# A post-norm layer (mLSTM and pooling mixer, squared-ReLU MLP): a pool of its own for the first norm's scale and bias, six weight loads held back, the second MLP product in another order

## The chip, the core and the metric

The kernel runs on one core of one Trainium2 chip. The metric is the device time of one execution in microseconds (us). The engines are TensorE (PE: matmuls, and transposes through the matmul array), VectorE (DVE), ScalarE (ACT), GpSimd (POOL) and SyncE (SP, which here only issues loads). Each runs its own list of instructions in order and waits for others by semaphores. DMA queues move data between HBM and the on-chip memory (SBUF); matmuls write to PSUM.

## What is computed

One layer over 1024 tokens of width 1024, all in float32:

```
u = x @ w_in                                  # q, k, v, gates, output gate, pooling columns
h = mLSTM(silu(conv(q)), silu(conv(k)), v, i, f)   # 4 heads x 128, a state carried from chunk to chunk
y_m = sigmoid(output gate) * layer_norm_per_head(h) * hn_g
y_p = (trailing means over 2/4/8/16 - p) @ w_pool * scale
x1 = layer_norm(ALPHA * x + concat(y_m, y_p) @ w_out, ln1_g, ln1_b)
out = layer_norm(ALPHA * x1 + square(relu(x1 @ w_ff1)) @ w_ff2, ln2_g, ln2_b)
```

`w_ff1` is 1024 x 4096, `w_ff2` 4096 x 1024.

## The kernel before, in words

Every matmul operand is split into a high part (a cast on ScalarE, L76) and a low part (a subtraction on VectorE, L77), and each product is three matmuls (L103 to L105, in `mm3`). A column block of 512 takes one such matmul a little over 0.23 us.

**Mixer.** Tokens come in two halves of 512 (`hf`), each of four chunks of 128. The projections run one after another, `proj_o` (output gate), `proj_p` (pooling), `proj_vg` (v and gates), `proj_qk`; beside them lie the tasks put off with `later`, run when `tick` reaches their due step. `mlstm_stages(c)` is a chunk in four steps: decay weights (`ng`, `si`) by GpSimd (L489, L499) and ScalarE (L491); q-k scores on TensorE (L496) and the transposed keys (L503), scaled values `vs` on GpSimd (L507); then the output (L516, L517), copied by ScalarE into `o` (L518), and the state's increment (L524), added on VectorE into `C` (L526 or L530), which the next chunk's L516 reads; on VectorE the norm of `o` to `y` (L535 to L549); last the transposes of `y` (L553). L496, L517 and L524 write PSUM tiles named `ml`, of which there are two. The output gate of a chunk is copied (L234), put through a sigmoid (L238) and multiplied with `hng` by GpSimd (L239). In what follows, "the first chunk's copy" is L518 for chunk 0.

Nearly all working tiles of the mixer (`hng`, `og`, `o`, `y`, `kt`, `vs`, `u`, ...) come from one ring, `bigp`, of 42 tiles: a new tile takes the slot of the oldest and its first writer waits for the last reader of what stood there. A scheduler of the framework puts each engine's instructions in order from these waits and its estimates of their times.

`out_proj` multiplies with `w_out` in two column halves and applies the first norm; for the last two chunks of a half VectorE does it in two steps, L637 (scale, `gs[0:2]`) and L643 (bias, `gs[2:4]`). The four tiles `gs1` (named `lngb`) are scale and bias, spread over partitions by a GpSimd DMA (L915), taken from `bigp`.

**MLP.** After the mixer `bigp` is closed and its room goes to a pool `fq` of 21 tiles. The two matrix products are done in blocks of 512 with seven block products in place of eight; `jobs` lists them as (r, ph, i): four rounds r, phase 0 (`w_ff1`) and 1 (`w_ff2`), and i in the order 1, 2, 5, 6, 3, 7, 4 in the first round. A job has 16 tile steps of three matmuls, 48 in all. `prep(n)` makes the operands of job n and calls `weights` for job n + 1 (n + 2 for n = 0): SyncE loads a base block (L732), GpSimd adds further blocks with accumulating DMAs (L735) where i needs a sum. Two tiles, p = 0 and 1, make a job's weights. `x1_transpose(1, ...)` transposes the last 512 tokens (L660, 32 transposes) at the second job, i = 2; job 3 (i = 5) needs them and a sum of two weight blocks.

Of the kernel before, what the change touches and what calls it, by code (L numbers as in the profile page):

```python
# [22 lines left out]
def trunk_layer(ctx: ExitStack, tc: tile.TileContext, x, w_in, b_gate, w_conv, hn_g,  # L23
# [24 lines left out]
    ps_tr = ctx.enter_context(tc.tile_pool(name="ps_tr", bufs=2, space=bass.MemoryType.PSUM))  # L48
    dram = ctx.enter_context(tc.tile_pool(name="dram", bufs=2, space=bass.MemoryType.DRAM))
    early = ExitStack()  # L50
    bigp = early.enter_context(tc.tile_pool(name="bigp", bufs=42))

    cnt = [0]
    anchor = [None]
# [8 lines left out]
    def sml(shape, tag, bufs=2):  # L63
        return small.tile(shape, F32, tag=tag, name=nm(tag), bufs=bufs)
# [11 lines left out]
        act.copy(hi, src)  # L76
        dve.tensor_tensor(lo, src, hi.bitcast(F32), ALU.subtract)  # L77

    def after(ins, anchor):
        tc.add_manual_dep(  # L80
            ins.ins, anchor.ins.name,
            mybir.DependencyInfo(mybir.DependencyClass.NoSync, mybir.DependencyReason.DATA),
            reason="start of the load")

    def wpiece(src, n, before=None):
# [294 lines left out]
    def gates_stages(hf):  # L380
        g8 = gt[hf]
        iv, fv = g8[:, :, 0:4], g8[:, :, 4:8]
        v3 = lambda t: t.rearrange("p (c h) -> p c h", h=4)
        af, u, lnu, t1 = (sml([P, 16], n) for n in ("g_af", "g_u", "g_ln", "g_t1"))
        lf = sml([P, 16], "g_lf")
        ab = sml([P, 2, 16], "g_ab")
        dve.scalar_tensor_tensor(v3(af), fv, -1.0, fv, op0=ALU.mult, op1=ALU.min)
        act.activation(af, af, AF.Exp)
        dve.tensor_scalar(u, af, 1.0, None, op0=ALU.add)
        act.activation(lnu, u, AF.Ln)  # L390
        dve.scalar_tensor_tensor(t1, u, -1.0, af, op0=ALU.add, op1=ALU.subtract)
        dve.reciprocal(u, u)
        dve.tensor_tensor(t1, t1, u, ALU.mult)
        dve.tensor_tensor(t1, lnu, t1, ALU.subtract)
        dve.scalar_tensor_tensor(v3(lf), fv, 0.0, v3(t1), op0=ALU.min, op1=ALU.subtract)
        yield
        pa = trps([P, 16])
        pe.matmul(pa, lhsT=tri, rhs=lf, start=True, stop=True)
        dve.tensor_copy(ab[:, 0, :], pa)
        dve.tensor_tensor(v3(ab[:, 1, :]), iv, v3(ab[:, 0, :]), ALU.subtract)  # L400
        yield
        pt = trps([16, 2, P])
        for i in range(2):
            pe.transpose(pt[:, i, :], ab[:, i, :], ident)
        abT = big([16, 2, P], name="g_abT")
        dve.tensor_copy(abT, pt)
        cm = big([16, P], name="g_cm")
        dve.tensor_tensor_scan(cm, zcol.to_broadcast([16, P]), abT[:, 1, :], -3.0e38, op0=ALU.add, op1=ALU.max)
        yield
        pr = trps([1, 2, 16])  # L410
        pe.transpose(pr[:, 0, :], abT[:, 0, P - 1:P], ident[:16, :16])
        pe.transpose(pr[:, 1, :], cm[:, P - 1:P], ident[:16, :16])
        row = sml([1, 2, 16], "g_row")
        dve.tensor_copy(row, pr)
        dve.tensor_tensor(row[:, 1, :], row[:, 1, :], row[:, 0, :], ALU.add)
        m = sml([1, 20], "g_m")
        gm = sml([1, 16], "g_gm")
        dve.tensor_copy(m[:, 0:4], mst)
        for c in range(TT):
            s, s2 = slice(4 * c, 4 * c + 4), slice(4 * c + 4, 4 * c + 8)  # L420
            dve.tensor_tensor(gm[:, s], row[:, 0, s], m[:, s], ALU.add)
            dve.tensor_tensor(m[:, s2], gm[:, s], row[:, 1, s], ALU.max)
        dve.tensor_copy(mst, m[:, 16:20])
        rr = sml([1, 2, 16], "g_rr")
        dve.tensor_tensor(rr[:, 0, :], row[:, 0, :], m[:, 4:20], ALU.subtract)
        dve.tensor_tensor(rr[:, 1, :], gm, m[:, 4:20], ALU.subtract)
        yield
        pb = trps([P, 2, 16])
        pe.matmul(pb.rearrange("p a b -> p (a b)"), lhsT=ones, rhs=rr.rearrange("p a b -> p (a b)"),
                  start=True, stop=True)  # L430
        so, ep = sml([P, 16], "g_so"), sml([P, 16], "g_ep")
        act.activation(so, pb[:, 1, :], AF.Exp)
        dve.tensor_tensor(ep, ab[:, 1, :], pb[:, 0, :], ALU.add)
        act.activation(ep, ep, AF.Exp)
        pm = trps([16, 1])
        pe.transpose(pm, m[:, 0:16], ident[:1, :1])
        mp = sml([16, 1], "g_mp")
        dve.tensor_copy(mp, pm)
        gs = big([16, 2, P], name="g_gs")
        dve.tensor_scalar(gs[:, 0, :], cm, mp, -1.0, op0=ALU.max, op1=ALU.mult)  # L440
        act.activation(gs[:, 1, :], gs[:, 0, :], AF.Exp, bias=mp)
        th = big([16, P], name="g_th")
        dve.scalar_tensor_tensor(th, gs[:, 0, :], 0.5 * math.log(P), abT[:, 0, :],
                                 op0=ALU.add, op1=ALU.subtract)
        act.activation(th, th, AF.Exp)
        yield
        pth = trps([P, 16])
        pe.transpose(pth, th, ident[:16, :16])
        thr = sml([P, 16], "g_thr")
        dve.tensor_copy(thr, pth)  # L450
        dr = dram.tile([2, 16, P], F32, tag="bounce", name=nm("bounce"))
        act.dma_start(dr.rearrange("a r t -> r a t"), gs)
        G[hf] = dict(so=so, ep=ep, b=ab, thr=thr, dr=dr)
# [196 lines left out]

    xq = {}

    def x1_transpose(hf, kbs, alloc):
        for kb in kbs:
            if kb % 2 == 0:
                xq[kb // 4, hf, kb % 4 // 2] = alloc()
            t = xq[kb // 4, hf, kb % 4 // 2]
            ps = trps([P, TT, P])
            for j in range(TT):
                pe.transpose(ps[:, j, :], z[hf * TT + j, kb // 4][:, (kb % 4) * P:(kb % 4 + 1) * P], ident)  # L660
            act.copy(t[:, kb % 2, :], ps.rearrange("p j t -> p (j t)"))

    def x_second(j):
# [17 lines left out]
    def quad(name="q"):  # L681
        return fq.tile([P, 2, 512], F32, tag="q", name=nm(name))
# [14 lines left out]

    banks = [lambda: mmps([P, 512]), aux]

    def product(L, R, ps, first, outer="k"):  # L700
        steps = [(p, kk) for p in C2 for kk in C2]
        its = [(s, m) for s in steps for m in range(4)] if outer == "k" else \
            [(s, m) for m in range(4) for s in steps]
        for (p, kk), m in its:
            s = slice(m * P, (m + 1) * P)
            anchor[0] = mm3(ps[m], L[p][0][:, kk, s], L[p][1][:, kk, s], R[p][0][:, kk, :], R[p][1][:, kk, :],
                            first and p == 0 and kk == 0, p == 1 and kk == 1, not first)
# [15 lines left out]

    grown = {}

    def weights(r, ph, i):
        parts = (WQ1, WQ2)[ph][i]
        for p in C2:
            t, have = grown.pop((r, ph, parts[:-1], p), (None, 0)) if len(parts) > 1 else (None, 0)
            if t is None:  # L730
                t = quad("w")
                sp.dma_start(t, w_source(r, ph, parts[0], p))  # L732
                have = 1
            for q in parts[have:]:
                pool.dma_start(t, w_source(r, ph, q, p), accum_op=ALU.add)  # L735
            grown[r, ph, parts, p] = (t, len(parts))
# [74 lines left out]
    def prep(n):  # L811
        r, ph, i = jobs[n]
        if n == 0:
            L, R = firsts[1], firsts["x"]
        elif n == 1:
            L, R = firsts[2], x_right(r, i)
        elif ph == 0:
            L, R = operands(r, ph, i), x_right(r, i)
        else:
            L, R = h_left(i), operands(r, ph, i)  # L820

        k = n + 1 + (n == 0)
        if n != 1 and k < len(jobs):
            weights(*jobs[k])
        return L, R

    def evict1(i, ps):
# [81 lines left out]
    proj_qk(1, 0)  # L909
    later(1, lambda: mlstm(1))  # L910
    proj_p(1)
    gs1 = [big([P, 512], name="lngb") for _ in range(4)]
    for e in range(4):
        src = (ln1_g, ln1_b)[e // 2][0:1, e % 2 * 512:(e % 2 + 1) * 512]
        after(pool.dma_start(gs1[e], src.to_broadcast([P, 512])), anchor[0])  # L915
# [3 lines left out]
    early.close()  # L919
    fq = ctx.enter_context(tc.tile_pool(name="fq", bufs=21, reuse_waits="tile"))  # L920

    ready = prep(0)
    open_ps = {}
    for n, (r, ph, i) in enumerate(jobs):
        L, R = ready
        if n == 1:
            x1_transpose(1, range(KB), lambda: quad("x1"))
        if n + 1 < len(jobs):
            ready = prep(n + 1)
        which = CHAIN[i]  # L930
        if i in FIRST:
            open_ps[which] = [banks[which ^ ph]() for _ in range(4)]
        ps = open_ps[which]
        if (r, ph, i) == (NR - 1, 1, 5):
            for v in (ln2_g, ln2_b):
                t = quad("lngb")
                after(pool.dma_start(t.rearrange("p e c -> p (e c)"), v.to_broadcast([P, 1024])), anchor[0])
                gb2.append(t)
        fin = r == NR - 1 and ph == 1 and i in (2, 3, 7, 4)
        product(L, R, ps, i in FIRST, "m" if fin else "k")  # L940
        if ph == 0:
            evict1(i, ps)
        else:
            evict2(i, ps, r)
# [25 lines left out]
```

## Time and profile before

| | |
|---|---|
| median of 3 runs | 1042.88 us (1039.37 to 1043.12) |
| profiled execution, its own time | 1042.8 us |
| its span in the profile | 1041.1 us |
| mean granted TensorE clock | 0.991 |
| busy: PE, DVE, ACT, POOL | 97%, 71%, 43%, 15% of the span |
| DMA | 141.20 MB, mean 136 GB/s |

A granted clock of 1.00 is 2.4 GHz, 0.50 is 1.2 GHz. A wait is put down to the instruction whose semaphore came last; "<-DVE z L643" means that VectorE's instruction of line 643 on the tile `z` ended it. Where nothing is said, times are us from the start of the span.

### The profile page before, as it was taken

The page shows a single profiled execution, that of the slowest core. Times are in us where ns is not written, and L with a number is a line of the kernel's source. Part 1 is how long each engine was busy: PE and PEld are TensorE (multiplying, and loading weights), DVE is VectorE, ACT ScalarE, POOL GpSimd, SP SyncE. Part 2 cuts the span into 40 slices and gives each one's busy share as a digit, 9 for nine tenths or more (in the row PEclk, how much of TensorE's full clock was granted, in tenths as well). Part 3 has the DMA queues.
Part 4 walks back from the last instruction along what each step waited for, and adds up shares of the span by engine and source line. Part 5 has one row for each costly group of instructions (what it writes and reads, how often), then busy time and mean ns, then how long its engine had stood idle before and what let it go on. Part 6 is the DMA issues. An engine that isn't in the chain of part 4 may idle for free.

```text
span 1041.1 us, 12565 instructions
## 1 busy us (share of the span) xinstructions
PE 1007.4 (97%) x4697; PEld 824.4 (79%) x4697; DVE 734.7 (71%) x1203; ACT 450.7 (43%) x644; POOL 155.4 (15%) x194
## 2 busy tenths in 40 slices
PE   7999999999989998899999999999999999999995
PEld 5898789887868887688888888888888888888884
DVE  5473864977898476768966478966478965478887
ACT  5334555547522134443333534333534333534363
POOL 2320002220330011400302001302001302000211
PEclk9999999999999999899999999999999999999998
DMA  8411503323531147993908953908953908902656
GB/s 294 152 63 41 163 22 92 123 81 101 182 83 58 44 111 233 294 302 92 162 1 180 283 200 64 162 1 185 290 191 62 162 1 187 298 1 42 122 101 203
DMA packets 63518, 141.20 MB, mean 136 GB/s; under 512 B 4620, under 2 KB 4704, under 8 KB 63456
## 3 DMA queue, kind: packets, MB, share of 16 engines
q1 hardware_dynamic: 41328, 91.04, 26.2%
q0 software_dynamic: 21744, 48.79, 23.9%
q8 instruction: 37, 0.61, 0.2%
q10 hardware_dynamic: 384, 0.56, 0.1%
q14 instruction: 25, 0.20, 0.1%
HBM read 126.18 MB, written 11.57 MB: 132 GB/s over the span
## 4 chain that ended last, share of the span: by engine, by line
PE 84%; DVE 8%; DMA 4%; ACT 2%; issue 1%; DVEq 0%; SPq 0%; ACTq 0%; POOLq 0%
PE mm L105 17%; PE mm L103 17%; PE mm L104 17%; PE tr L103 5%; PE tr L104 5%; PE tr L105 5%; PE ml L103 5%; PE ml L104 5%; PE ml L105 5%; DMA w<-in_w_ff_dram 2%; DMA xraw<-in_x_dram 1%; DVE wlo L77 1%; DVE ol L77 1%; DMA xres<-in_x_dram 1%; PE tr L177 1%
## 5 line engine op out<-in xcount | busy, mean ns | idle before, releaser
L77 DVE TENSOR_TENSOR ol<-w,oh 128x1024 fp32r<-128x1024 f32 x112 | 135.7, 1222 | 97.1 <-ACT oh L76 97.0
L76 ACT CAST oh<-w 128x1024 fp32r<-128x1024 f32 x112 | 116.6, 1047 | 153.2 <-PE mm L104 51.1
L103 PE MATMUL mm<-oh,oh 128*128 128x512 f32 x448 | 176.4, 394 | 0.0
L104 PE MATMUL mm<-ol,oh 128*128 128x512 f32 x448 | 176.2, 393 | 0.0
L105 PE MATMUL mm<-oh,ol 128*128 128x512 f32 x448 | 176.2, 394 | 0.0
L735 POOL DMA_DIRECT2D w<-in_w_ff_dram x64 | 77.0, 1287 | 512.8 <-DVE ol L77 476.9
L105 PEld LDWEIGHTS mm<-oh,ol 128*128 128x128 f32 x448 | 84.1, 188 | 19.7
L104 PEld LDWEIGHTS mm<-ol,oh 128*128 128x128 f32 x448 | 84.1, 188 | 19.6
L103 PEld LDWEIGHTS mm<-oh,oh 128*128 128x128 f32 x448 | 84.1, 188 | 19.6 <-DVE h L837 0.2
L103 PE MATMUL ml<-oh,oh 128*128 128x512 f32 x224 | 88.7, 397 | 1.8 <-ACT oh L76 1.8
L103 PE MATMUL tr<-oh,oh 128*128 128x512 f32 x224 | 89.0, 398 | 1.0 <-DVE h L837 0.9
L104 PE MATMUL ml<-ol,oh 128*128 128x512 f32 x224 | 88.6, 396 | 0.9 <-DVE ol L77 0.9
L105 PE MATMUL tr<-oh,ol 128*128 128x512 f32 x224 | 88.9, 397 | 0.0
L104 PE MATMUL tr<-ol,oh 128*128 128x512 f32 x224 | 88.9, 397 | 0.0
L105 PE MATMUL ml<-oh,ol 128*128 128x512 f32 x224 | 88.5, 395 | 0.0
L77 DVE TENSOR_TENSOR ol<-xs,oh 128x1024 fp32r<-128x1024 f32 x42 | 51.4, 1223 | 46.0 <-ACT oh L76 45.7
L76 ACT CAST oh<-h 128x1024 fp32r<-128x1024 f32 x40 | 41.8, 1047 | 79.9 <-PE ml L104 24.6
L76 ACT CAST oh<-xs 128x1024 fp32r<-128x1024 f32 x42 | 44.0, 1048 | 61.6 <-PE ml L104 37.5
L77 DVE TENSOR_TENSOR wlo<-raw,whi 128x1024 fp32r<-128x1024 f32 (+1 forms) x44 | 54.8, 1246 | 17.5 <-ACT whi L76 9.9
L76 ACT CAST whi<-raw 128x1024 fp32r<-128x1024 f32 (+1 forms) x44 | 46.1, 1053 | 34.8 <-PE mm L104 13.8
L103 PE MATMUL mm<-xT,whi 128*128 128x512 f32 x144 | 57.3, 398 | 0.1
L104 PE MATMUL mm<-xT,whi 128*128 128x512 f32 x144 | 57.0, 396 | 0.0
(276 smaller groups left out, 1992.9 us busy)
## 6 DMA issues: line engine op xcount, KB each, us to landing
w<-in_w_ff_dram POOLq DMA_DIRECT2D x64, 512.0 KB, 7.2
w<-in_w_ff_dram SPq DMA_DIRECT2D x58, 512.0 KB, 6.7
xs<-xs SPq DMA_DIRECT2D x42, 512.0 KB, 5.5
raw<-in_w_in_dram SPq DMA_DIRECT2D x28, 512.0 KB, 4.3
xs<-x POOLq DMA_DIRECT2D x12, 512.0 KB, 7.4
raw<-in_w_in_dram SPq DMA_DIRECT2D x8, 520.0 KB, 5.4
raw<-in_w_out_dram SPq DMA_DIRECT2D x8, 512.0 KB, 3.3
xres<-in_x_dram SPq DMA_DIRECT2D x8, 512.0 KB, 3.6
```

The source lines that it names most:

```text
L76: act.copy(hi, src)
L77: dve.tensor_tensor(lo, src, hi.bitcast(F32), ALU.subtract)
L103: pe.matmul(ps, lhsT=lh, rhs=rh, start=start, stop=False, skip_group_check=grow)
L104: pe.matmul(ps, lhsT=lh, rhs=rl, start=False, stop=False, skip_group_check=grow)
L105: return pe.matmul(ps, lhsT=ll, rhs=rh, start=False, stop=stop, skip_group_check=grow)
L177: pe.transpose(ps[:, a, b, :], raw[:, b, kc * P:(kc + 1) * P], ident)
L735: pool.dma_start(t, w_source(r, ph, q, p), accum_op=ALU.add)
```

## The change

Three edits. `gs1` moves from the ring to a pool `gsp` of four tiles; the ring has 39 tiles instead of 42, and ten small tiles of the gate computation have one buffer instead of two. `weights` gets an argument `hold`: with it, SyncE issues a base load only when that matmul has ended; it is the last matmul of job n - 3 in the calls from `prep(n + 1)` for n = 3 to 6. And job 1 (i = 2) is done in parts: the two output tiles m = 1, 3 for three of their four steps (18 matmuls), then the 32 transposes tied behind them, the operands of job 2, the rest of m = 1, 3, then m = 0, 2.

```diff
-    bigp = early.enter_context(tc.tile_pool(name="bigp", bufs=42))
+    bigp = early.enter_context(tc.tile_pool(name="bigp", bufs=39))
+    gsp = early.enter_context(tc.tile_pool(name="gsp", bufs=1))
...
-    def after(ins, anchor):
+    def after(ins, anchor, wait=False):
         tc.add_manual_dep(
             ins.ins, anchor.ins.name,
-            mybir.DependencyInfo(mybir.DependencyClass.NoSync, mybir.DependencyReason.DATA),
+            mybir.DependencyInfo(mybir.DependencyClass.Sync if wait else mybir.DependencyClass.NoSync, mybir.DependencyReason.DATA),
             reason="start of the load")
...
-        af, u, lnu, t1 = (sml([P, 16], n) for n in ("g_af", "g_u", "g_ln", "g_t1"))
-        lf = sml([P, 16], "g_lf")
+        af, u, lnu, t1 = (sml([P, 16], n, 1) for n in ("g_af", "g_u", "g_ln", "g_t1"))
+        lf = sml([P, 16], "g_lf", 1)
...
             for j in range(TT):
-                pe.transpose(ps[:, j, :], z[hf * TT + j, kb // 4][:, (kb % 4) * P:(kb % 4 + 1) * P], ident)
+                t0 = pe.transpose(ps[:, j, :], z[hf * TT + j, kb // 4][:, (kb % 4) * P:(kb % 4 + 1) * P], ident)
+                if start is not None:
+                    after(t0, start)
...
-    def product(L, R, ps, first, outer="k"):
-        steps = [(p, kk) for p in C2 for kk in C2]
-        its = [(s, m) for s in steps for m in range(4)] if outer == "k" else \
-            [(s, m) for m in range(4) for s in steps]
+    STEPS = [(p, kk) for p in C2 for kk in C2]
+
+    def product(L, R, ps, first, outer="k", ms=range(4), steps=STEPS):
+        its = [(s, m) for s in steps for m in ms] if outer == "k" else \
+            [(s, m) for m in ms for s in steps]
...
-                sp.dma_start(t, w_source(r, ph, parts[0], p))
+                load = sp.dma_start(t, w_source(r, ph, parts[0], p))
+                if hold is not None:
+                    after(load, hold, True)
...
-            weights(*jobs[k])
+            weights(*jobs[k], ends[n - 3] if 3 <= n <= 6 else None)
...
-    gs1 = [big([P, 512], name="lngb") for _ in range(4)]
+    gs1 = [gsp.tile([P, 512], F32, name=f"lngb{e}") for e in range(4)]
...
-        if n == 1:
-            x1_transpose(1, range(KB), lambda: quad("x1"))
-        if n + 1 < len(jobs):
+        if n + 1 < len(jobs) and n != 1:
             ready = prep(n + 1)
...
-        product(L, R, ps, i in FIRST, "m" if fin else "k")
+        if n == 1:
+            product(L, R, ps, True, "k", (1, 3), STEPS[:3])
+            x1_transpose(1, range(KB), lambda: quad("x1"), anchor[0])
+            ready = prep(2)
+            product(L, R, ps, True, "k", (1, 3), STEPS[3:])
+            product(L, R, ps, True, "k", (0, 2))
+        else:
+            product(L, R, ps, i in FIRST, "m" if fin else "k")
+        ends.append(anchor[0])
```

**On ScalarE, in the mixer.** The place of the first chunk's copy of its output into the tile `o`. Before, it stands right behind the copies of `v`, and the casts of the weights of `proj_o(1)` (`whi`) follow:

```order
L505 COPY kt_1681<-tr_1676 128x512
L285 COPY v_274_1685<-mm_1687 128x2x128
L285 COPY v_274_1685<-mm_1688 128x2x128
L518 COPY o_1740<-ml_1741 128x258
L518 COPY o_1740<-ml_1745 128x258
L76 CAST whi_1891<-raw_1889 128x1024
L76 CAST whi_1897<-raw_1895 128x1024
L76 CAST whi_2220<-raw_2218 128x1024
L76 CAST whi_2226<-raw_2224 128x1024
```

After (the line numbers are one higher), it stands behind the last copies and sigmoids of the output gate:

```order
L235 COPY og_2209<-mm_2073 128x512
L239 ACTIVATE og_2209<-og_2209 128x512
L235 COPY og_2209<-mm_2074 128x512
L77 CAST whi_2530<-raw_2528 128x1024
L239 ACTIVATE og_2209<-og_2209 128x512
L519 COPY o_1743<-ml_1744 128x258
L519 COPY o_1743<-ml_1748 128x258
L506 COPY kt_1812<-tr_1807 128x512
L286 COPY v_296_1825<-mm_1827 128x2x128
```

The two rows `o<-ml` moved from ahead of eight casts of weights and four copies and four sigmoids of `og` to behind them.

**On TensorE, in the mixer.** The first state increment (`ml<-vs,kt`) and the scores of the next chunk (`ml<-qk,qk`). Before, they stand at the end of a tile pair of `proj_vg(1)`, and that projection's next 48 matmuls (`mm<-whi,xT`) follow:

```order
L517 MATMUL ml_1741<-v_103_593,ng_1599 128x129 x2
L517 MATMUL ml_1745<-v_103_593,ng_1599 128x129 x2
L503 MATMUL tr_1804<-ident,qk_1168 128x128
L524 MATMUL ml_1749<-vs_1683,kt_1681 128x129 x2
L524 MATMUL ml_1753<-vs_1683,kt_1681 128x129 x2
L503 MATMUL tr_1804<-ident,qk_1168 128x128 x3
L496 MATMUL ml_1797<-qk_870,qk_1168 128x128 x4
L103 MATMUL mm_1824<-whi_1521,xT_918 128x256
L104 MATMUL mm_1824<-wlo_1522,xT_918 128x256
L105 MATMUL mm_1824<-whi_1521,xT_918 128x256
```

After, they stand inside the first tile pair of `proj_qk(1, 0)`, and the second chunk's output (`ml<-C,si`) begins right behind the scores:

```order
L104 MATMUL mm_2246<-xT_923,whi_2229 128x512
L525 MATMUL ml_1752<-vs_1686,kt_1684 128x129 x2
L525 MATMUL ml_1756<-vs_1686,kt_1684 128x129 x2
L105 MATMUL mm_2246<-xT_923,whi_2229 128x512
L106 MATMUL mm_2246<-xT_923,wlo_2230 128x512
L104 MATMUL mm_2245<-xT_924,whi_2229 128x512
L497 MATMUL ml_1800<-qk_873,qk_1171 128x128 x4
L517 MATMUL ml_1946<-C_212,si_1610 128x129
L105 MATMUL mm_2245<-xT_924,whi_2229 128x512
L106 MATMUL mm_2245<-xT_924,wlo_2230 128x512
L104 MATMUL mm_2246<-xT_924,whi_2229 128x512
L518 MATMUL ml_1946<-v_112_667,ng_1609 128x129
```

The increment moved past the rest of `proj_vg(1)` and the whole of `proj_o(1)`; between the steps of the first four chunks there now lie mostly three to six matmuls of the projection.

**On TensorE, at the start of the MLP.** The end of the first product (`mm`) and what follows. Before, eight transposes of the last tokens (`tr<-ident,z`):

```order
L104 MATMUL mm_3817<-ol_3728,oh_3404 128x512
L105 MATMUL mm_3817<-oh_3727,ol_3405 128x512
L660 MATMUL tr_3873<-ident,z_3288 128x128
L660 MATMUL tr_3873<-ident,z_3291 128x128
L660 MATMUL tr_3873<-ident,z_3366 128x128
L660 MATMUL tr_3873<-ident,z_3369 128x128
L660 MATMUL tr_3879<-ident,z_3288 128x128
L660 MATMUL tr_3879<-ident,z_3291 128x128
L660 MATMUL tr_3879<-ident,z_3366 128x128
L660 MATMUL tr_3879<-ident,z_3369 128x128
L103 MATMUL ml_3951<-oh_3802,oh_3782 128x512
L104 MATMUL ml_3951<-ol_3803,oh_3782 128x512
```

After, the second product's tiles `ml`:

```order
L105 MATMUL mm_3821<-ol_3731,oh_3407 128x512
L106 MATMUL mm_3821<-oh_3730,ol_3408 128x512
L104 MATMUL ml_3877<-oh_3806,oh_3785 128x512
L105 MATMUL ml_3877<-ol_3807,oh_3785 128x512
L106 MATMUL ml_3877<-oh_3806,ol_3786 128x512
L104 MATMUL ml_3879<-oh_3806,oh_3785 128x512
L105 MATMUL ml_3879<-ol_3807,oh_3785 128x512
L106 MATMUL ml_3879<-oh_3806,ol_3786 128x512
L104 MATMUL ml_3877<-oh_3806,oh_3785 128x512
L105 MATMUL ml_3877<-ol_3807,oh_3785 128x512
```

Eighteen such matmuls now stand ahead of the first transpose; before, they stood behind the first eight.

## Rows read from the trace of the kernel before

**Rows 1.** The page, part 1: busy us of each engine, share of the span, instructions.

```profile
PE 1007.4 (97%) x4697; PEld 824.4 (79%) x4697; DVE 734.7 (71%) x1203; ACT 450.7 (43%) x644; POOL 155.4 (15%) x194
```

**Rows 2.** Stretches: length, busy us (instructions) of each engine, granted clock, DMA share, GB/s.

```profile
177.87:207.00 29.13, 27.12 (x173) 23.95 (x172) 26.23 (x87) 14.98 (x24) 8.15 (x8) 1.00 0.34 109
207.00:340.00 133.00, 127.98 (x654) 105.58 (x653) 109.62 (x320) 58.73 (x108) 27.28 (x24) 0.99 0.32 100
265.00:310.00 45.00, 41.63 (x217) 34.15 (x215) 43.01 (x108) 14.77 (x30) 15.24 (x15) 1.00 0.46 140
440.00:1000.00 560.00, 560.00 (x2418) 453.65 (x2417) 406.00 (x417) 234.13 (x260) 71.35 (x61) 1.00 0.57 142
```

**Rows 3.** Timeline of TensorE: start, us, line, operation, in brackets the wait and its releaser.

```profile
195.91 0.68 PE L524 MATMUL ml<-vs,kt 128*128 128x129 f32 x4 [2.00 <-ACT o L518]
...
215.37 1.16 PE L496 MATMUL ml<-qk,qk 128*128 128x128 f32 x8 [0.95 <-DVE C L530]
...
310.69 0.66 PE L553 MATMUL tr<-ident,y 128*128 128x128 f32 x4 [3.21 <-DVE y L549]
...
404.05 0.33 PE L660 MATMUL tr<-ident,z 128*128 128x128 f32 x1 [1.72 <-DVE z L643]
...
405.38 0.76 PE L660 MATMUL tr<-ident,z 128*128 128x128 f32 x5 [0.99 <-DVE z L643]
...
422.50 0.51 PE L103 MATMUL ml<-oh,oh 128*128 128x512 f32 x1 [1.83 <-ACT oh L76]
...
423.95 0.50 PE L104 MATMUL ml<-ol,oh 128*128 128x512 f32 x1 [0.94 <-DVE ol L77]
...
425.68 0.80 PE L103 MATMUL tr<-oh,oh 128*128 128x512 f32 x1 [0.91 <-DVE h L837]
```

**Rows 4.** Timeline, ScalarE and GpSimd: first output copy, last gate copy, last products with hng.

```profile
177.87 0.82 ACT L518 COPY o<-ml 128x258 f32<-128x258 f32 x2
...
221.69 0.60 ACT L234 COPY og<-mm 128x512 f32<-128x512 f32 x1
...
222.89 4.45 POOL L239 TENSOR_TENSOR og<-og,hng 128x512 f32<-128x512 f32 x2 [8.12 <-ACT og L238]
```

**Rows 5.** Stretch 177.87 to 221.7, instructions on the tile ml (the chunk chain) alone.

```profile
177.87:221.70 43.83, 11.24 (x84) 9.98 (x82) 5.09 (x13) 2.00 (x6) 1.00 0.33 103
```

**Rows 6.** VectorE's groups from 177.87 to 221.7: line, shapes, count, busy us, mean ns, idle.

```profile
L77 DVE TENSOR_TENSOR wlo<-raw,whi 128x1024 fp32r<-128x1024 f32 x7 | 8.6, 1225 | 0.2 <-ACT whi L76 0.2
```

**Rows 7.** Timeline, VectorE, SyncE, ScalarE: end of the first norm, weight loads, the late cast.

```profile
393.05 2.72 DVE L637 SCALAR_TENSOR_TENSOR z<-z,l_mv,lngb 128x512 f32<-128x512 f32 x4
...
403.24 2.74 DVE L643 SCALAR_TENSOR_TENSOR z<-z,l_s,lngb 128x512 f32<-128x512 f32 x4
...
406.06 3.48 SPq L732 DMA_DIRECT2D w<-in_w_ff_dram  x7
...
420.45 1.05 ACT L76 CAST oh<-w 128x1024 fp32r<-128x1024 f32 x1 [4.94 <-DMA w<-in_w_ff_dram]
```

**Rows 8.** DMA issues at 388.5, 400.03 and 410.44: operation, count, KB, us to landing.

```profile
w<-in_w_ff_dram SPq DMA_DIRECT2D x1, 512.0 KB, 9.8
...
w<-in_w_ff_dram POOLq DMA_DIRECT2D x1, 512.0 KB, 6.1
...
w<-in_w_ff_dram POOLq DMA_DIRECT2D x1, 512.0 KB, 10.0
```

**Rows 9.** Two stretches at the start of the MLP, columns as in group 2.

```profile
402.33:412.00 9.67, 6.95 (x38) 5.62 (x38) 4.84 (x7) 3.18 (x6) 1.56 (x2) 1.00 0.81 223
424.44:431.27 6.83, 5.92 (x15) 4.43 (x14) 6.05 (x8) 2.29 (x3) 2.11 (x3) 0.50 1.10 272
```

**Rows 10.** Timeline, VectorE and GpSimd around 201: an operation beside GpSimd's addition.

```profile
200.87 0.16 DVE L471 TENSOR_TENSOR r_t<-r_y 128x4 f32<-128x4 f32 x1
...
201.46 1.15 DVE L471 TENSOR_TENSOR r_t<-r_y 128x4 f32<-128x4 f32 x1
...
201.28 1.30 POOL L489 TENSOR_TENSOR ng<-ng,mask 128x512 f32<-128x512 f32 x1 [5.12 <-DMA ng<-bounce]
```

More of the change, by code (lines that the diff above doesn't have):

```diff
@@ L412, in gates_stages @@
         pe.transpose(pr[:, 1, :], cm[:, P - 1:P], ident[:16, :16])
-        row = sml([1, 2, 16], "g_row")
+        row = sml([1, 2, 16], "g_row", 1)
         dve.tensor_copy(row, pr)
         dve.tensor_tensor(row[:, 1, :], row[:, 1, :], row[:, 0, :], ALU.add)
-        m = sml([1, 20], "g_m")
-        gm = sml([1, 16], "g_gm")
+        m = sml([1, 20], "g_m", 1)
+        gm = sml([1, 16], "g_gm", 1)
         dve.tensor_copy(m[:, 0:4], mst)
@@ L423, in gates_stages @@
         dve.tensor_copy(mst, m[:, 16:20])
-        rr = sml([1, 2, 16], "g_rr")
+        rr = sml([1, 2, 16], "g_rr", 1)
         dve.tensor_tensor(rr[:, 0, :], row[:, 0, :], m[:, 4:20], ALU.subtract)
@@ L436, in gates_stages @@
         pe.transpose(pm, m[:, 0:16], ident[:1, :1])
-        mp = sml([16, 1], "g_mp")
+        mp = sml([16, 1], "g_mp", 1)
         dve.tensor_copy(mp, pm)
@@ L651, in trunk_layer, with x1_transpose @@
     xq = {}
-    def x1_transpose(hf, kbs, alloc):
+    def x1_transpose(hf, kbs, alloc, start=None):
         for kb in kbs:
@@ L724, in trunk_layer, with weights @@
     grown = {}
-    def weights(r, ph, i):
+    def weights(r, ph, i, hold):
         parts = (WQ1, WQ2)[ph][i]
@@ L920, in trunk_layer @@
     fq = ctx.enter_context(tc.tile_pool(name="fq", bufs=21, reuse_waits="tile"))
+    open_ps, ends = {}, []
     ready = prep(0)
-    open_ps = {}
     for n, (r, ph, i) in enumerate(jobs):
         L, R = ready
-        if n == 1:
-            x1_transpose(1, range(KB), lambda: quad("x1"))
-        if n + 1 < len(jobs):
+        if n + 1 < len(jobs) and n != 1:
             ready = prep(n + 1)
```

## The prediction

> **What bounds the kernel now.** I read the page's busy shares first, then a table of stretches, then every wait of TensorE, then what stands ahead of the waits on the other engines. TensorE is busy 97% of the span [rows 1], and from 440 to 1000 us it never idles: 2418 matmuls in 560 us, 0.2316 us each [rows 2]. So only the stretches before 440 and the tail can give or take anything, and the change touches two of them.
>
> The first is the start of the MLP. There TensorE waits 1.72 and 0.99 us for L643 (the last tokens of the first norm), then 1.83 and 0.94 us for operands of the third product and 0.91 for a PSUM tile to be read out (L837) [rows 3]; from 424.44 the clock granted is 0.50 (1.2 GHz) for 6.83 us [rows 9].
>
> The second is the token mixer from 178 to 340 us. Its waits of TensorE look small: 2.00, 0.95 and 3.21 us [rows 3]. But VectorE is nearly full: 43.01 of 45 us from 265 to 310 [rows 2]. That is the reserve to watch.
>
> **Part 1, MLP start, the gains.** (a) The transposes of the last tokens now stand behind 18 matmuls of the second product, 18 x 0.2316 = 4.2 us [rows 2]. In the kernel before they came right behind the first product and waited 1.72 + 0.99 = **2.71 us** for L643, which began at 403.24 and ran 2.74 us [rows 3, 7]. TensorE reached that place about 402.3; with 18 matmuls ahead it arrives at 406.5, after L643's end at 405.98. The cover is those 18 matmuls; they need operands split from loads long landed. If one were late, the same 2.7 us would be paid there.
>
> (b) The second half of the third product's weights (L732) waited for the last reader of the "bias" tile: it went out at 406.06, the moment L643's chain let go of the slot, at the head of a burst of seven loads [rows 7]. Its accumulating load, issued at 410.44, took 10.0 us beside that burst, where the one before it, issued at 400.03, took 6.1 [rows 8]. The cast on ScalarE then waited until 420.45 [rows 7] and TensorE 1.83 + 0.94 + 0.91 = **3.68 us** in all [rows 3]. With the scale and bias in a pool of their own the ring's slots beneath are laid out differently, and this load waits only for L637, which began at 393.05 and ran 2.72 us [rows 7]: it goes out at about 396. If it then takes as long as the slowest load near it (9.8 us [rows 8]) and its accumulate the full 10.0, the tile is there at 416, casts (about 2 us) done at 418. TensorE would want it at 422.50 - 1.83 - 2.71 = 418. So even at worst little is left; with an accumulate of 6.1 [rows 8] nothing. I take 3.68 gained, at worst 3.
>
> (c) Without those waits there is no reason for the fall to half clock: 15 matmuls took 5.92 us of engine time there [rows 9] where 15 x 0.2316 = 3.47 are needed, so **2.45 us** come back. If the clock falls all the same, none.
>
> (d) The held loads are six: two each for the sixth, seventh and eighth product, each pair held until the end of the product four before its own. Queued behind them on SyncE are later weight loads and the re-loads of token sums, none of which is due for many products. The earliest pair leaves when the second product ends, at about 418, lands by 428 and is accumulated by 438 at the slowest durations of [rows 8], and its split is due beside the fifth product, which starts two products of 48 x 0.2316 = 11.1 us later, at 440. I cost it at nothing; were a pair late, TensorE would wait as it did for the third product's, 1.83 us. What the hold protects, the accumulate, is in (b).
>
> Sum of part 1: -(2.71 + 3.68 + 2.45) = **-8.8 us**; at worst -4 (no clock gain, 0.7 us of new waiting, 1.5 us of late operands).
>
> A rule speaks against (a). The rows first: over 402.33 to 412.00, with 2.71 us of waiting and most of the transposes, the granted clock stayed 1.00 (2.4 GHz) [rows 9]. The Trainium skill, "TensorE: Matmul & The Clock Gate", Part 4 (PE-mode transpose), says transposes don't count as a busy TensorE for the clock. By that rule the 32 transposes that now lie in four groups between matmuls would bring the low clock back and take the 2.45 us of (c) away, for a total of -6.4; the trace here disagrees, with 1.00 over the same transposes.
>
> **Part 2, the mixer, the price.** The room for the new pool is taken from the ring: 39 slots instead of 42, and single buffers for ten small gate tiles. Here the order of ScalarE tells what this does: the first chunk's output copy (L518 before) stood before the weight casts of the output gate's projection, and now stands after that projection's last sigmoid, since its tile takes the slot of `hng`, which GpSimd reads last in L239. Before, that copy ran at 177.87; the projection's last copy ran at 221.69 and the last two `hng` products ended at 222.89 + 4.45 = 227.34 [rows 4]. Both accumulator tiles of the chunk chain are held until the copy, so TensorE's next chunk step waits with it, and four chunks' steps now stand inside two projection tiles.
>
> TensorE itself loses nothing at first: it does the projection without the chunk steps, some 84 matmuls of up to 11.24 us, and without the waits 2.00 and 0.95 [rows 3, 5], so the projection ends some 13 us earlier, near 208.7, and the copy runs near 211. What is lost is VectorE's time. From 177.87 to 340 it works 26.23 + 109.62 = 135.85 us [rows 2], of which 8.6 us are the seven low parts of weights up to 221.7 [rows 6], which now come ahead of the copy. The other 127.3 us start at 211 instead of 177.87.
> - Lower bound: at the fullest rate seen, 43.01/45 = 0.956 [rows 2], 127.3 us take 133, so the work ends at 344 where it ended at 340: **+4**.
> - Upper bound: at the mean rate of 207 to 340, 109.62/133 = 0.824 [rows 2], it takes 154 and ends at 365: **+25**.
>
> Between them I take the middle, **+15**. The lower end would need VectorE never to wait; but a chunk's state update (L530), the next chunk's matmuls and ScalarE's copy follow each other, and the waits already seen go to each of them in turn (ScalarE's copy 2.00, L530 0.95, `y` 3.21 [rows 3]). The upper end is unlikely since a fuller queue leaves VectorE fewer idle moments than the mean of that stretch. The 1.7 us or so that the half clock at the 3.21 us wait costs now may come again at another place; I count it as unchanged.
>
> The move of the four scale and bias loads on GpSimd's queue, ahead of small copies, and fewer table loads on ScalarE cost nothing on the path: ScalarE is busy 43%, GpSimd 15% [rows 1]. The single gate buffers cost nothing either: the second half's gates come a round of projections after the first half's, whose tiles are read out by then; if a wait were left there it would delay the second half's chunks alone, inside the +25.
>
> **Total.** The profiled run took 1042.8 us, like the median of 1042.88. 1042.8 - 8.8 + 15 = **1049**.
>
> **The rivals.** *Late chain absorbed.* VectorE's spare time takes it all: +0 to +4 in the mixer, the gain at the start stays: 1034 to 1038. For it: VectorE idles 133 - 109.6 = 23 us from 207 to 340 [rows 2]. Against: it idles 33 us in its place while waiting for the slot. It decides for faster as soon as the mixer costs under 3.6 us. That the ring of 39 does not bind, and the change does only what its words say, ends here too.
>
> *Contention in the squeeze.* GpSimd's elementwise work of the chunks now lies beside a full VectorE. In the trace L471 took 0.16 us at 200.87 and 1.15 at 201.46, beside GpSimd's 1.30 us from 201.28 [rows 10]. Six to ten more such meetings cost 6 to 10 us: mixer +21 to +25, total 1055 to 1059. The Trainium skill, "SBUF — State Buffer", Who interferes with whom, calls this pair of ports an exclusive lock, the later one waiting; these rows agree.
>
> *The start does not gain.* The accumulate meets other traffic in its new place, or the held loads are late, and only 2.71 comes back: 1042.8 + 15 - 2.7 = 1055.
>
> *The transposes bring the low clock.* If the granted clock falls beside the four groups of transposes as it did at 424.44, the 2.45 us of (c) stay lost: 1042.8 + 15 - 6.4 = 1051.4. Against it stands the 1.00 over most of the same transposes [rows 9]. It is the rule of the page named above.
>
> **How the numbers follow.** Chances: forecast, mixer +10 to +20 with the whole gain (1044 to 1054), 0.53; absorbed or nearly (1034 to 1043) 0.23; contention 0.12; start without gain 0.07; low clock 0.05. Some 0.5% (5.2 us) is about what a measurement of this kernel can tell from no change, so faster means below 1037.6 and slower above 1048.1. Of the absorbed case two thirds are faster: 0.16. Of the forecast 0.33 and of the other three nearly all (0.22) are slower: 0.55. Same 0.29. The range reaches from the absorbed case's upper half to contention: 1037 to 1058.
>
> **What would show it.** In the new profile: the first `o` copy on ScalarE near 211 and no chunk matmul between 180 and 205; VectorE over 90% busy from 210 to 270; TensorE waits there of over half a microsecond, ten or more, for VectorE; the wait for `y` over 3 us; out_proj's first matmul later by some 15. Then no wait for L643, the second weight load of the third product out some 10 us earlier against its neighbours, and no low clock near 425. I am wrong if TensorE's waits from 178 to 340 add up to under 10 us, or if the operands of the third product are still late.

## The result, and the profile after

The changed kernel takes **1047.9 us** (median of six runs, 1047.41 to 1049.61), the kernel before 1042.24 beside it: ratio **1.006**, 95% interval 1.0046 to 1.0073. It is slower by about the forecast's amount. Its profiled execution took 1048.05 us by its own time, with a span of 1046.3. In this part its lines stand one or a few higher than those of before (L518 is L519, L643 is L644, L732 is L736, L837 is L843).

The page, engine by engine (busy us, share of the span, instructions):

```profile
PE 1010.0 (97%) x4697; PEld 823.2 (79%) x4697; DVE 727.1 (69%) x1203; ACT 443.2 (42%) x638; POOL 156.2 (15%) x194
```

It reads like [rows 1] and tells nothing; the stretches do. The table compares both traces by work instead of by the clock: how much later than in the kernel before the same one of the split matmuls, counted from the start, begins.

| place (time in the kernel before) | after minus before, us |
|---|---|
| up to 171 | +0.3 to +0.5 |
| 218 | -13.8 |
| 252 | +5.3 |
| 305 | +9.2 |
| 330 to 391 (`out_proj`) | **+14.0** |
| 433 (third product) | **+3.8** |
| 489 to the end | **+5.4** |

So the mixer cost 14.0, the start of the MLP gave 10.2 back, and 1.6 came on top past 433, where nothing was forecast.

**The mixer.** Stretches of the changed kernel (columns as in [rows 2]: PE, PEld, DVE, ACT, POOL busy us with instructions, granted clock, DMA share, GB/s):

```profile
178.00:210.00 32.00, 32.00 (x168) 26.66 (x167) 9.97 (x9) 14.62 (x19) 5.27 (x5) 1.00 0.37 117
210.00:255.00 45.00, 39.62 (x224) 31.68 (x223) 40.48 (x182) 20.00 (x39) 9.62 (x9) 0.98 0.27 81
255.00:285.00 30.00, 27.96 (x135) 22.37 (x133) 18.38 (x30) 17.50 (x38) 12.82 (x12) 0.98 0.36 121
300.00:325.00 25.00, 16.87 (x80) 12.95 (x80) 24.14 (x61) 6.12 (x15) 8.83 (x6) 0.92 0.18 64
178.00:354.00 176.00, 160.20 (x827) 130.06 (x826) 128.36 (x406) 69.92 (x129) 37.32 (x33) 0.97 0.29 93
```

From 178 to 210 TensorE never idles and VectorE does 9 things in 32 us. Then VectorE has 40.48 of 45 us full, and at the end 24.14 of 25, while TensorE idles a third of that time. The same work of the kernel before lies in 178 to 340; over it:

```profile
178.00:340.00 162.00, 154.97 (x824) 129.39 (x823) 135.72 (x405) 73.57 (x131) 35.44 (x31) 0.99 0.33 101
```

TensorE idled 162 - 154.97 = 7.03 us there and 176 - 160.20 = 15.80 now: 8.8 of the 14 are idle time. The other 5.2 are longer matmuls; 2.4 of these are half clock, below. TensorE's waits (us in total, times, longest):

```profile
PE tr L554 <- DVE y L550: 6.6, 1, 6.6
PE mm L105 <- DVE wlo L78: 1.8, 2, 1.1
PE ml L497 <- DVE C L531: 1.6, 2, 1.4
PE ml L517 <- POOL si L500: 1.5, 2, 1.2
PE tr L504 <- DVE g_ab L400: 1.2, 1, 1.2
PE tr L437 <- DVE g_ep L434: 0.8, 1, 0.8
```

Five of the six are for VectorE, and `y`, the last of a half's chain, doubled from the 3.21 of [rows 3]. The first chunk's copy on ScalarE (start, duration, instruction, idle time before it and what ended that) stood at 177.87 in [rows 4] and is now the moment GpSimd's last product with `hng` is done:

```profile
211.57 0.65 ACT L519 COPY o<-ml 128x258 f32<-128x258 f32 x2 [1.40 <-POOL og L240]
```

The clock fell to 0.50 (1.2 GHz) twice in the mixer, for 3.41 and 6.83 us:

```profile
252.76:256.17 3.41, 3.41 (x12) 2.74 (x11) 3.41 (x10) 1.79 (x3) 0.00 (x0) 0.50 0.37 138
321.02:327.85 6.83, 4.79 (x21) 4.42 (x22) 4.55 (x9) 1.94 (x6) 2.94 (x2) 0.50 0.04 15
```

Half of 3.41 + 4.79 busy us is 4.1 lost. The kernel before lost half of one such stretch, 1.7, at its 3.21 us wait:

```profile
311.80:315.21 3.41, 3.41 (x19) 3.41 (x18) 1.94 (x4) 0.38 (x2) 0.00 (x0) 0.50 0.13 25
```

**The start of the MLP.** Between 400 and 440 TensorE now has no wait, where [rows 3] has five, and no half clock, where [rows 9] has 0.50. Landmarks on VectorE and SyncE, and a stretch:

```profile
406.96 2.73 DVE L638 SCALAR_TENSOR_TENSOR z<-z,l_mv,lngb 128x512 f32<-128x512 f32 x4
415.88 2.74 DVE L644 SCALAR_TENSOR_TENSOR z<-z,l_s,lngb 128x512 f32<-128x512 f32 x4
409.71 0.37 SPq L736 DMA_DIRECT2D w<-in_w_ff_dram  x1
```

```profile
413.00:440.00 27.00, 26.92 (x130) 21.37 (x130) 22.81 (x27) 14.44 (x21) 10.11 (x11) 1.00 0.79 208
```

L638 is 13.9 us later than L637 in [rows 7], as the table says. The weight load follows it at once, at 409.71; moved back by the 13.9 that is 395.8. In the kernel before it followed L643.

**Past it.** TensorE has two new waits, 0.67 and 0.49 us, for a PSUM tile that VectorE has yet to read out, and VectorE (last four rows) has no gap there:

```profile
476.69 0.47 PE L104 MATMUL mm<-oh,oh 128*128 128x512 f32 x1 [0.67 <-DVE h L843]
479.52 0.50 PE L104 MATMUL mm<-oh,oh 128*128 128x512 f32 x1 [0.49 <-DVE h L843]
...
472.45 2.35 DVE L78 TENSOR_TENSOR ol<-x,oh 128x1024 fp32r<-128x1024 f32 x2
474.73 1.22 DVE L78 TENSOR_TENSOR ol<-h,oh 128x1024 fp32r<-128x1024 f32 x1
475.86 1.88 DVE L843 TENSOR_TENSOR h<-h,mm 128x512 f32<-128x512 f32 x3
477.65 1.22 DVE L845 SCALAR_TENSOR_TENSOR h<-h 128x1024 f32<-128x1024 f32 x1
```

### The profile page after: what moved, and what is told of

It reads as the page before. It is cut to its first block, busy times and chain, and to the rows that moved or that the text cites. A ratio compares the mean times of both kernels' runs of the same rounds, so it can differ in the third digit from the quotient of the medians.

```text
span 1046.3 us, 12573 instructions
## 1 busy us (share of the span) xinstructions
PE 1010.0 (97%) x4697; PEld 823.2 (79%) x4697; DVE 727.1 (69%) x1203; ACT 443.2 (42%) x638; POOL 156.2 (15%) x194
## 4 chain that ended last, share of the span: by engine, by line
PE 81%; DVE 8%; DMA 4%; issue 3%; ACT 2%; POOL 1%; SPq 0%; DVEq 0%; POOLq 0%; ACTq 0%
PE mm L104 17%; PE mm L105 17%; PE mm L106 17%; PE ml L104 4%; PE ml L105 4%; PE ml L106 4%; PE tr L105 4%; PE tr L106 4%; PE tr L104 4%; DMA w<-in_w_ff_dram 3%; DVE ol L78 1%; DMA raw<-in_w_in_dram 1%; PE ml L518 1%; PE ml L517 1%; DVE ps L345 0%
```

## The experiments

All in one table first: the median and its ratio to the kernel before on the same chip, and how much later the same split matmul begins than in the kernel before, at the three places of the table above (391: end of the mixer; 433: third product; 489: past the held loads).

| run | median, us | ratio (95%) | 391 | 433 | 489 |
|---|---|---|---|---|---|
| the change | 1047.9 | 1.006 (1.0046 to 1.0073) | +14.0 | +3.8 | +5.4 |
| e3, ring 39 alone | 1050.59 | 1.0075 (1.0046 to 1.0103) | +12.8 | +7.0 | +8.4 |
| e4, ring 40 alone | 1037.96 | 0.9958 (0.9942 to 0.9974) | +3.9 | -4.6 | -3.8 |
| e11, ring 41 alone | 1037.99 | 0.9954 (0.9939 to 0.9968) | +2.6 | -3.2 | -3.1 |
| e9, change with less on VectorE | 1040.87 | 0.9989 (0.9977 to 1.0) | +6.0 | -4.0 | -1.9 |
| e10, before with less on VectorE | 1033.07 | 0.9919 (0.9888 to 0.995) | -3.5 | -10.7 | -10.7 |
| e1, pools alone | 1049.61 | 1.0063 (1.0042 to 1.0083) | +12.2 | +3.4 | +3.6 |
| e7, order alone | 1042.92 | 1.0012 (1.0001 to 1.0023) | +2.2 | +1.9 | +1.8 |
| e5, hold alone | 1039.18 | 0.998 (0.997 to 0.9991) | +1.2 | -6.2 | -2.0 |
| e2, hold and order | 1039.71 | 0.9972 (0.9959 to 0.9984) | -0.4 | -6.1 | -3.8 |
| e6, change without hold | 1046.83 | 1.0058 (1.0037 to 1.0079) | +12.3 | +4.1 | +4.1 |
| e8, ring 41 and order | **1033.4** | **0.9926** (0.9903 to 0.9949) | -0.6 | -10.6 | -10.2 |

### Is the mixer's price the size of the ring?

**e3**, the kernel before with three slots fewer and nothing else:

```diff
-    bigp = early.enter_context(tc.tile_pool(name="bigp", bufs=42))
+    bigp = early.enter_context(tc.tile_pool(name="bigp", bufs=39))
```

> The kernel before with 39 ring tiles instead of 42 and nothing else changed. Theory (the ring delays the first chunk's copy and VectorE fills up): +14 in the mixer, about 1056. Rival (the single gate buffers or the earlier loads of scale and bias cost it): within 1 us of the kernel before, 1042.

Measured: +12.8 at 391. The summary of the `o` copies between 170 and 230 us in this run (count, shortest, median and longest in ns, first and last start in us):

```profile
L518 ACT COPY o<-ml x6: 374/378/380, 210.2 to 228.0; 128x258 f32<-128x258 f32 x6
```

The ring alone, without the pool and with two gate buffers as before, moves the copy from 177.87 to 210.2 and costs what the change costs. The single gate buffers and the earlier loads of scale and bias are out as causes. The median is 5 us under the expected 1056, since the start of the MLP gained 12.8 - 7.0 = 5.8 here too: the ring of 39 frees the load by itself.

**e4**, one slot more:

```diff
-    bigp = early.enter_context(tc.tile_pool(name="bigp", bufs=42))
+    bigp = early.enter_context(tc.tile_pool(name="bigp", bufs=40))
```

> The kernel before with 40 ring tiles. Theory (a step: only when the first chunk's copy falls on the slot of hng does it move behind the output gate): it keeps its place with 40, 0 to +4, 1042 to 1046. Rival (each lost tile costs its share of 14): +9, 1051.

Measured: the copy is at 178.5, as the same summary says of this run:

```profile
L518 ACT COPY o<-ml x6: 352/380/407, 178.5 to 216.0; 128x258 f32<-128x258 f32 x6
```

The mixer costs 3.9, inside the 0 to 4 expected. Of this 1.8 are a longer wait (3.77 us, ended at 198.92; 2.00 in [rows 3]) and 1.7 the half clock behind it (half of 3.42 us from 200.04); a new idle 1.38 us at 280 and a longer half clock from 312.68 add some 2.7, shorter waits for L530 and L518 take off 1.5. The median is below the expected range because the start gained 8.5, which I had not expected of this run. So the price is no share per slot but a step: between 40 and 39 slots the copy's tile falls upon the slot of `hng`, whose last reader is far behind it.

### Is it VectorE that the late chain waits for?

**e9** and **e10** cut the same work of VectorE, two of three steps of an iteration in the chunk norm (`rsqrt_eps`), out of the change and out of the kernel before.

```diff
-        for _ in range(3):
+        for _ in range(1):
```

> The changed kernel with one Newton step in place of three in the head norm's inverse root (two thirds of L472 to L474 left out, so the norm is less exact): 48 short VectorE operations fewer. Theory (VectorE is what the mixer waits for after the delayed copy): the mixer gets 6 to 9 us shorter than in the changed kernel, about 1040. Rival (the delayed chain costs by its waits between engines, VectorE only along for it): no more than the same cut gives on the kernel before.

> The same cut on the kernel before, as the measure for e9_newton_after. Theory (VectorE is full only near 300): the mixer 2 to 4 us shorter, 1038 to 1040. Rival: as much as on the changed kernel, 6 to 9.

Measured at 391: 14.0 - 6.0 = 8.0 us saved in the change, 3.5 in the kernel before. In the change the wait for `y` fell from 6.61 to 4.02 and the mean clock over 178 to 340 rose from 0.97 to 0.99. Against e1 and e6, which have the change's mixer and cost 12.2 and 12.3, the saving is 6.2 to 6.3. So the same cut is worth about twice as much where the chain starts late, which speaks for VectorE's work as what is short there; the cut also shortens the path of the last norm itself, and that part is in both figures. e10 has a second effect that I had not planned: its weight loads left in one burst of eight from 385.46, so the third product's late load was not late, and 7.2 us came back at the start. Its median therefore prices the cut too high; the stage at 391 doesn't.

### Which part does what at the start of the MLP?

**e1**, the pools alone (with the single buffers of the ten gate tiles):

```diff
-    bigp = early.enter_context(tc.tile_pool(name="bigp", bufs=42))
+    bigp = early.enter_context(tc.tile_pool(name="bigp", bufs=39))
+    gsp = early.enter_context(tc.tile_pool(name="gsp", bufs=1))
...
-    gs1 = [big([P, 512], name="lngb") for _ in range(4)]
+    gs1 = [gsp.tile([P, 512], F32, name=f"lngb{e}") for e in range(4)]
```

> The pools alone (ring of 39, scale and bias in their own pool, single gate buffers); no held loads, the second product as before. Theory (the ring makes the mixer's cost, the early weight load makes most of the start's gain): mixer +14, the waits 1.83 + 0.94 + 0.91 and the low clock near 425 gone (-6.1), the wait for L643 (2.71) stays: about 1050. Rival (the hold is what frees the accumulating load): the late cast stays, about 1056.

**e7**, the new order of the second product alone:

```diff
-        product(L, R, ps, i in FIRST, "m" if fin else "k")
+        if n == 1:
+            product(L, R, ps, True, "k", (1, 3), STEPS[:3])
+            x1_transpose(1, range(KB), lambda: quad("x1"), anchor[0])
+            ready = prep(2)
...
```

> The new order of the second product alone, on the kernel before. Theory: the wait of 2.71 for L643 goes, but the cast of the third product's weights still ends where it did, so the same 2.7 us are waited there instead: 1042, within 1. Rival (the terms add): -2.7, 1039.5.

Measured: e1 gains 12.2 - 3.4 = 8.8 us at the start; the waits for L644 stay (1.2 us in two), those for late operands and the half clock are gone. e7 gains 0.3: it removes the waits for L643, and TensorE then waits for the same late load all the longer. TensorE's row, and ScalarE's cast that it waits for:

```profile
424.60 0.79 PE L103 MATMUL ml<-oh,oh 128*128 128x512 f32 x1 [4.56 <-ACT oh L76]
...
422.56 1.04 ACT L76 CAST oh<-w 128x1024 fp32r<-128x1024 f32 x1 [7.89 <-DMA w<-in_w_ff_dram]
```

4.56 us where [rows 3] has 1.83: the 2.71 of the removed wait went into the next one. The late load decides; the order gains only behind it.

**e5**, the hold alone, and **e2**, hold and order together:

```diff
-                sp.dma_start(t, w_source(r, ph, parts[0], p))
+                load = sp.dma_start(t, w_source(r, ph, parts[0], p))
+                if hold is not None:
+                    after(load, hold, True)
...
-            weights(*jobs[k])
+            weights(*jobs[k], ends[n - 3] if 3 <= n <= 6 else None)
```

> The held loads alone, on the kernel before. Theory: the accumulating load shortens from 10 to some 6 us, so the waits for the third product's operands shrink by about 3 us, and later the held loads cost some 2 us near 470, as in e2_hold_order: together about -1, 1041. Rival (the hold is free): -3 to -6, 1036 to 1039.

> The held loads and the new order of the second product on the ring of 42, scale and bias in the ring. Theory: mixer unchanged, 2.71 gained by the order, and the accumulating load, though its base still leaves at 406, takes some 6 us instead of 10 without the burst, so that the cast comes in time: -8.8, about 1033.5. Rival (the own pool is needed for the late cast): only -2.7 to -4, 1038 to 1039.5.

**e6**, the change with no load held:

```diff
-            weights(*jobs[k], ends[n - 3] if 3 <= n <= 6 else None)
+            weights(*jobs[k], None)
```

> The changed kernel without the held loads. Theory (the early load alone removes the late cast, and the hold costs the 1.16 us of waits near 476): mixer +14, start -10, no waits near 476: 1046. Rival (the hold protects the accumulating load): the cast is late again by 2 to 4 us, 1050 to 1052.

Measured: with the load late, the hold is worth something: e5 gains 1.2 + 6.2 = 7.4 at 433, since the accumulating load then has no burst beside it (5.7 us to landing, 10.0 in [rows 8]). But it gives 4.2 back by 489. This is so wherever it stands: from 433 to 489 the change loses 1.6, e5 4.2, e2 2.3 and e9 2.1; the eight kernels without it lose at most 1.4, six of them under 0.5. e5's waits of TensorE past 440:

```profile
PE mm L103 <- DVE h L842: 1.5, 2, 1.0
PE mm L103 <- ACT oh L76: 0.9, 1, 0.9
PE mm L104 <- DVE ol L77: 0.8, 1, 0.8
```

They are for casts and subtractions of weights, and for PSUM tiles not read out since those are queued ahead on VectorE. e2 missed its 1033.5 and came to 1039.71, the number of its rival: with hold and order TensorE still waits 1.0 us for a PSUM tile and 0.9 for a low part of the third product, half clock follows for 3.42 us from 420.65, and the start gains 6.1 - 0.4 = 5.7, less than the hold alone. Where the pools have already mended the load, the change against e6, the hold gains 2.0 at the start (10.2 against 8.2) and loses 1.6 behind it. Whether it helps or costs there on the whole, the medians do not settle: 1.006 against 1.0058, with intervals that overlap.

### The gain without the price

**e11**, one slot fewer, the load's slot thus another, the copy's not yet `hng`'s; **e8**, the same with the new order:

```diff
-    bigp = early.enter_context(tc.tile_pool(name="bigp", bufs=42))
+    bigp = early.enter_context(tc.tile_pool(name="bigp", bufs=41))
```

> The kernel before with 41 ring tiles and nothing else. Theory (the slots alone bring the early load; the order then only hides what is left of the wait for L643, some 1.3 us): mixer +0, start -8.5, 1034 to 1035. Rival (the order and the early load each bring half): 1037 to 1039.

> The kernel before with 41 ring tiles and the new order of the second product; no own pool, no held loads. Theory (the start's gain comes from which slots the scale, bias and weights share, and the mixer's cost only from the step at 39): mixer +1 to +2, start -9 to -10, 1034. Rival (the own pool is needed for the start's gain): late cast stays, 1042 to 1044.

Measured: e8 is the fastest of all that were run with the whole computation, 1033.4 us, 0.7% under the kernel before and 14.5 us under the change. Its mixer is that of before, and from 400 to 440 TensorE does not idle:

```profile
400.00:440.00 40.00, 39.92 (x187) 31.96 (x186) 32.91 (x34) 20.44 (x29) 14.67 (x18) 1.00 1.04 282
```

Without the order, e11 keeps the waits for L643 (2.6 us) and a half clock at 408.5, and gains 5.8 at the start where I had expected some 8.5; its median lies in the range of the rival, 1037 to 1039. The stretch:

```profile
408.50:411.91 3.41, 3.41 (x11) 2.64 (x10) 1.23 (x1) 0.79 (x2) 0.58 (x1) 0.51 1.12 214
```

So the early load is worth 5.8 (e11) to 8.8 (e1), order and load together 8.2 (e6, with one wait of 1.0 us left) and 10.0 (e8). The order's own share behind the load is thus 4.2 on the ring of 41 and nothing that can be told (-0.6) beside the new pool. The traces show where the 4.2 lies: e11 waits 2.6 us for L643 and loses half of 3.41 to the half clock behind it, 4.3 in all; e1 waits 1.2 there with no half clock, and e6 has 1.2 of other waits in its place. Why that wait is 2.6 in e3 and e11 and 1.2 to 1.4 in e1 and e4 stays open. A pool of its own for scale and bias is not needed for it: rings of 40 and 41 slots free the load as well.

## Why the prediction was right, point by point

- **The mixer, +15, measured +14.0.** The mechanism is shown: copy at 211.57 (forecast 211), no chunk work of VectorE before it, waits for VectorE after it, and the ring alone reproduces it (e3). The sum behind the number was right by two errors that cancelled. It put 127.3 us of VectorE work behind the copy, at a rate between 0.824 and 0.956. The trace has 128.36 - 9.97 = 118.4 us from 210 to 354, at 118.4/144 = 0.82. The work shrank, for one thing since small instructions met GpSimd less often, below; the rate was the upper bound's. VectorE idled from 255 to 285 (18.38 of 30 us busy), and there not for the reason I had given (state, matmul and copy in turn): its two long waits were 6.18 us for the decay weights from ScalarE (L492) and 4.37 for the transposed gates (L449). There is luck in the 14.0 too. e1 and e6 have the same mixer and cost 12.2 and 12.3; up to 247 their traces keep within 0.3 us of the change's, and they have no half clock at 252.76. So 1.7 of the 14.0 is a half clock that the same code does not always get.
- **Half clock in the mixer, "counted as unchanged": wrong.** 4.1 us against 1.7. This and 8.8 of idle time make 11.2 of the 14.0; the other 2.8 are matmuls a little longer in many places, which no row singles out.
- **The marks of it.** VectorE over 90% from 210 to 270: 90% to 255, less behind. Ten or more waits over half a microsecond for VectorE: six, and two for other engines. `y` over 3 us: 6.61. TensorE's idle time over 10 us: 15.8.
- **(a) and (b), the waits at the start, -2.71 and -3.68: right.** None of the five is left. The load went out at 395.8 by the time of before, forecast 396, and followed L638 as said. But the two terms were not independent, as the sum had them: e7 shows that (a) is worth nothing while (b) is late. Nor is 2.71 shown as its worth in the change: without the order, e1 waits only 1.2 for L644.
- **(c), the half clock at the start, -2.45: right.** 1.00 from 413 to 440. The start gave 10.2 where the three terms have 8.84; of the rest, half of the 5.92 busy us of [rows 9] would be 2.96 for (c) in place of 2.45, and what is left is not in one place.
- **(d), the held loads, "at nothing": wrong by the 1.6 us that appeared past 433.** In the code it is `prep(n)`, n from 3 to 6, whose loads wait for the end of job n - 3. The first held pair left at 431.71 and 432.13 and landed at 440.93 and 442.06, as forecast (428 and the 13.9 us of the mixer). Its accumulating loads did not keep to it: they were issued at 445.78 and 446.53, behind four `xs<-x` issues of GpSimd that wait for VectorE, took 11.3 and 14.1 us where I had put 10.0 as the slowest, and landed at 457.12 and 460.65, forecast 452. In e6, without the hold, the same two took 8.9 and 12.1. ScalarE's cast of the second one, in the change and then in e6, and VectorE's read-out of the PSUM tiles in e6, for which TensorE does not wait there:

```profile
460.73 1.05 ACT L77 CAST oh<-w 128x1024 fp32r<-128x1024 f32 x1 [1.00 <-DMA w<-in_w_ff_dram]
```

```profile
459.32 1.05 ACT L77 CAST oh<-w 128x1024 fp32r<-128x1024 f32 x1 [1.41 <-DMA w<-in_w_ff_dram]
474.45 1.87 DVE L843 TENSOR_TENSOR h<-h,mm 128x512 f32<-128x512 f32 x3
```

  Both come 1.4 us later in the change (the read-out at 475.86), and from 463.24 to there VectorE has no gap. So two steps failed: the accumulating loads were put too short, and I looked at arrival alone, asking whether the held pairs land before they are due. They do; but VectorE has to subtract their low parts and is then late in emptying the PSUM tiles. I had named 1.83 as the price of a late pair; the four kernels with the hold paid 1.6 to 4.2.
- **The single gate buffers: right,** e3 costs about the same without them.
- **The rivals.** *Late chain absorbed* fell: VectorE's spare time was spent while waiting. *Contention in the squeeze* fell the other way: the small product that took 0.16 or 1.15 us in [rows 10] had these sums over the mixer of before and then of the change (busy us, mean ns, idle us before):

```profile
L471 DVE TENSOR_TENSOR r_t<-r_y 128x4 f32<-128x4 f32 x24 | 5.9, 247 | 0.5
```

```profile
L472 DVE TENSOR_TENSOR r_t<-r_y 128x4 f32<-128x4 f32 x24 | 3.8, 160 | 0.5
```

  The median of the 24 is 162 and 161 ns, the longest 1220 and 165: the long ones are gone. There were two, at 201.46 and 305.30, and both ran beside an operation of GpSimd; none of the other 22, and none of the 24 in the change, did. The Trainium skill, "SBUF — State Buffer", Who interferes with whom, describes the shared port as a lock; that there is a price agrees with [rows 10], but here the long meetings became fewer and not more. *The start does not gain* fell with its 10.2 us. *Transposes bring the low clock* fell with the 1.00 from 413 to 440, with the transposes among the matmuls. The Trainium skill, "TensorE: Matmul & The Clock Gate", Part 4 (PE-mode transpose), named in the prediction, says that transposes do not count as a busy TensorE for the clock; here four groups of eight, each of 1.0 to 1.2 us between matmuls, did not bring it down. Longer stretches of transposes were not tested.

In sum: +14.0 - 10.2 + 1.6 = +5.4, by the medians +5.7, forecast +6.2.

## What to carry to other kernels

Ask of a smaller ring which reader each slot now waits for, not how many slots it lost: 41 and 40 slots cost the mixer nothing to 3.9 us and 39 cost 12 to 14, since one early tile fell upon one with a late reader. Of two waits in a row on the path, cost the second with the first removed: the order alone moved 2.7 us from one to the next and won nothing. And a load that is held back must be costed by the loads that then run beside it and by the work that its arrival puts on another engine's queue, not only by whether it arrives in time.

## What the runs showed of the hardware that was not expected

- The same wait of TensorE is followed by half clock in one kernel and not in another. Both e8 and e11 wait for the `o` copy at 195 to 197 (2.35 and 2.41 us); the stretches around it, e8 first, then e11:

```profile
194.00:200.00 6.00, 3.82 (x25) 3.49 (x26) 5.28 (x23) 2.78 (x8) 2.56 (x3) 1.00 0.13 46
```

```profile
196.92:200.33 3.41, 3.25 (x12) 2.99 (x13) 2.69 (x15) 0.77 (x3) 1.05 (x1) 0.50 0.02 8
```

  e7 and e5 fell to half clock there too, with waits of 2.0 us, the kernel before and e2 did not with the same. It is worth about 1.6 us (half of 3.25) and is most of the +1.2, +2.2 and +2.6 at 391 of e5, e7 and e11. The 1.7 between the change and e1 or e6 is of the same kind. With one trace of each, differences of that size in the column cannot be put down to the edit.
- A chain moved closer together on a full VectorE had less work, not more: 128.36 us for 406 instructions where 405 took 135.72. The row of the small product above shows one part of it, 2.1 us, which is two long meetings with GpSimd; that GpSimd's work is the cause of the rest was not tested.
